# A decoder block: the rotation table's chain of the first half recorded twelve products sooner, and one convolved row's low part taken on VectorE

## The chip, the cores and the metric

The kernel runs on one core of a Trainium2 chip. The metric is the device time of one execution in microseconds (us), as the median of several runs. TensorE (PE in the profile, PEld for its weight loads) does the matrix products, VectorE (DVE), ScalarE (ACT) and GpSimd (POOL) do what is elementwise, and SyncE (SP) issues most transfers. ScalarE's queue issues some transfers too. Each engine carries out its instructions in the order in which they were recorded, and it waits where an operand or a buffer isn't ready yet.

## What is computed

The reference is one residual decoder block over a sequence of 2048 tokens of width 1024, in float32. What matters here, cut from it:

```python
h = rms_norm(x, g_norm[l]) * (1.0 + scale[:, None, :]) + shift[:, None, :]
proj = h @ w_in[l]
x_rnn, z_rnn, q, k, v, z_attn, g_r, g_a = jnp.split(proj, IN_SPLITS, axis=-1)
xc = causal_depthwise_conv(x_rnn, conv_w[l], conv_b[l])
hr = rg_lru(xc, w_a[l], b_a[l], w_x[l], b_x[l], lam[l], positions)
qh = apply_partial_rope(q.reshape(B, S, N_HEADS, HEAD_DIM), cos, sin)
kh = apply_partial_rope(k.reshape(B, S, N_HEADS, HEAD_DIM), cos, sin)
...
ang = positions.astype(jnp.float32)[..., None] * inv_freq
cos = jnp.cos(ang)[:, :, None, :]
sin = jnp.sin(ang)[:, :, None, :]
```

After the projection come a convolution of width 4 and a gated recurrence on one branch, attention with three dilations on the other, and a merge with two more projections.

## The kernel before, in words

**Products.** Every float32 matrix product is made of three products of two parts. An operand's high part is its value rounded to the matrix engine's format (`hi_act`, a copy on ScalarE, line 160), and the low part is the rest (`lo_pool`, a subtraction on GpSimd, line 166, or `lo_dve`, the same on VectorE, line 169). The three products are high by high, high by low and low by high (`mm3`).

**Halves and pairs.** The projection is made in two halves of 1024 tokens, `f` = 0 and 1. In each half the columns of `w_in` are worked through in pairs of 128-column blocks, and each pair takes seven products instead of eight, by a Strassen scheme (`strassen`). A product is twelve matmuls into one of the PSUM tiles X, Z, W, V or Y. Its order is X, then the last product of the pair before, into that pair's V, then Z, W, V, X again, and Y. The tiles come free by evictions: u1 is X's copy on ScalarE (line 391), and it has to be done before the second product into X starts. The sums with u2 and u3 leave by VectorE (`total`, line 461), and V has to be read before the next product into V.

**What sets the order.** Nothing is scheduled by a tool in this stage: the work of a pair is recorded in the order of the program, and after each product the program records what was set down for that product's number (`run_late`, with the tables `late` and `after_prod`, and `pump` for the weight operands). The weights of a product are loaded on SP's queue into five R tiles, summed on VectorE (lines 290, 291, 299, 304) and split into S tiles on ScalarE and GpSimd four products ahead; ScalarE's queue stores each S tile for the second half.

**The recurrence.** Eight of the pairs in a half are those of the recurrence (`recurrent`, m = 0 to 7). Their X parts go through the steps of `x_part`, at fixed lags in products: the convolution's first tap on ScalarE (line 974), three more on VectorE (980), the split of the convolved row xc into xh (160) and xl (166), the gates' six matmuls from it into the tiles pg, two sigmoids, decay, exponentials, a square root (1013), the scan on VectorE (1018) and the product with z (1023). The split is recorded two products after its start, and the gates' matmuls five after it. `j` is the column block of 512 tokens in the half. The pairs between those of the recurrence belong to the gates (`gate_pairs`, with a sigmoid in line 1235 or 1237 and, for z, a product in line 1242) or to the part of q and k that isn't rotated (`plain_pairs`).

**The rotation table.** `rotary_tables(rp, f)` sets down the chain that makes the cosines and sines of the half: a small load of the positions on SP (1047), a conversion (1054), the angles (1057), two reductions of the angle by multiples of two pi (1063 and 1070, on tiles kk and an of 128 by 128), a clamp, four sine activations on ScalarE with their own table (1084), a transposition on VectorE (1088), and eight stores to the scratch tabD on SP's queue (1092), in two groups of four. One step goes with each product, from product number `TABLES` of the half on. The two tiles of 128 by 512 that hold the result come from the ring `ev` in the first half, and so do the tiles in which the evicted gates wait for their stores. The table is read from tabD when the half's last pairs, the rotated ones, begin.

Of the kernel before, what the change touches and what calls it, by code (L numbers as in the profile page):

```python
# [11 lines left out]
F32R = mybir.dt.float32r  # L12
# [25 lines left out]
REBUILT = 20  # L38
NEG = 1e30

TABLES = 24

KV = (2, 3), (4, 3), (4, 3), (4, 3)

# [46 lines left out]
def decoder_block(ctx, tc, x, c, positions, g_norm, w_mod, b_mod, w_in, b_gate, conv_w, conv_b,  # L91
# [4 lines left out]
    def T(pool, shape, dt, tag, **kw):  # L96
        cnt[0] += 1
        return pool.tile(shape, dt, tag=tag, name=f"{tag}_{cnt[0]}", **kw)
# [60 lines left out]
    def hi_act(o, i):  # L159
        nc.scalar.activation(o, i, AF.Copy)  # L160
# [4 lines left out]
    def lo_pool(o, i, h):  # L165
        nc.gpsimd.tensor_tensor(o, i, h.bitcast(F32), ALU.subtract)  # L166
# [57 lines left out]
    n_prod, late, after_prod = [0], {}, {}  # L224
# [230 lines left out]
    def total(dst, ps, u, perm=lambda ap: ap):  # L455

        with tc.high_priority():
            if u is None:
                nc.scalar.activation(dst, perm(ps[:]), AF.Copy)
            else:  # L460
                nc.vector.tensor_tensor(dst, perm(ps[:]), perm(u[:]), ALU.add)  # L461
# [466 lines left out]
    def recurrent(rp, bigr, f, m):  # L928
# [33 lines left out]
        def x_part(j, ps, u):  # L962
            xr = T(rp, [P, 3 + CH], F32, "xr", bufs=2)
            total(xr[:, 3:].rearrange("p (j r) -> p j r", r=4), ps, u, nat)
            v = {}

            def new(tag, dt=F32, bufs=1):
                v[tag] = T(rp, [P, CH], dt, tag, bufs=bufs)
                return v[tag][:]

            def tap():
                nc.scalar.activation(xr[:, 0:3], xtail[:, m, :], AF.Copy)
                nc.scalar.activation(xtail[:, m, :], xr[:, CH : CH + 3], AF.Copy)
                nc.scalar.activation(new("xc", bufs=2), xr[:, 0:CH], AF.Identity, scale=cw(0),  # L974
                                     bias=par[:, C_CB + m : C_CB + m + 1])

            def taps():
                xc = v["xc"][:]
                for i in range(1, 4):
                    nc.vector.scalar_tensor_tensor(xc, xr[:, i : i + CH], cw(i), xc, ALU.mult, ALU.add)  # L980

            def split():
                hi_act(new("xh", F32R), v["xc"][:])
                lo_pool(new("xl", F32R), v["xc"][:], v["xh"][:])

            def gates():
                for gt in range(2):
                    v["p", gt] = T(pg, [P, CH], F32, "pg")
                    mm3(v["p", gt][:], w["h"][:, gt, :], w["l"][:, gt, :], v["xh"][:], v["xl"][:])

            def sigmoids():
                for gt, dst, cb in ((0, new("y", bufs=2), C_BA), (1, new("gi"), C_BX)):
                    nc.scalar.activation(dst, v["p", gt][:], AF.Sigmoid, bias=par[:, cb + m : cb + m + 1])

            def decay():
                gi, y = v["gi"][:], v["y"][:]
                nc.gpsimd.tensor_tensor(gi, gi, v["xc"][:], ALU.mult)
                nc.vector.scalar_tensor_tensor(y, y, sp8[:, m : m + 1], bigr[:, j * CH : (j + 1) * CH],
                                               ALU.mult, ALU.add)

            def exponentials():
                y, a, t = v["y"][:], new("a"), new("t")
                nc.scalar.activation(t, y, AF.Tanh)
                nc.scalar.activation(a, y, AF.Exp, scale=-1.0)
                nc.scalar.activation(y, a, AF.Square)

            def root():
                t = v["t"][:]
                nc.vector.scalar_tensor_tensor(t, v["y"][:], 1.0, t, ALU.add, ALU.mult)

            def square_root():
                t = v["t"][:]
                nc.scalar.activation(t, t, AF.Sqrt)

            def scan():
                y, t = v["y"][:], v["t"][:]
                nc.vector.tensor_tensor(t, t, v["gi"][:], ALU.mult)
                nc.vector.tensor_tensor_scan(y, v["a"][:], t, htail[:, m : m + 1], ALU.mult, ALU.add)

            def finish():  # L1020
                nc.scalar.activation(htail[:, m : m + 1], v["y"][:, CH - 1 : CH], AF.Copy)
                z4 = zs[j][:].rearrange("p (r j) -> p r j", r=4)
                nc.vector.tensor_tensor(z4, v["y"][:].rearrange("p (j r) -> p r j", r=4), z4, ALU.mult)

            def store():
                c0 = f * HALF + j * CH
                nc.sync.dma_start(yaT[m * P : (m + 1) * P, c0 : c0 + CH], zs[j][:])

            if j == 0:
                start[0] = n_prod[0]  # L1030
            steps_after(start[0] + 7 * j, (
                (0, tap), (1, taps), (2, split), (GATES, gates), (GATES + 1, sigmoids), (GATES + 2, decay),
                (GATES + 3, exponentials), (GATES + 4, root), (GATES + 5, square_root), (GATES + 6, scan),
                (GATES + 7, finish), (GATES + 7, store)))
# [6 lines left out]
    def rotary_tables(rp, f):  # L1041

        v = {}

        def angles():
            pi = T(rp, [P, 2, 4], I32, "pi")
            nc.sync.dma_start(pi[:], positions[0].rearrange("(n j r) -> j n r", n=NB, r=4)[:, 2 * f : 2 * f + 2, :])
            v["pi"] = pi
            for tag in ("an", "kk", "co"):
                v[tag] = T(rp, [P, 8, 16], F32, tag)  # L1050

        def convert():
            v["pf"] = T(rp, [P, 8], F32, "pf")
            nc.vector.tensor_copy(v["pf"][:], v["pi"][:].rearrange("p n r -> p (n r)"))

        def products():
            nc.vector.tensor_tensor(
                v["an"][:], v["pf"][:].unsqueeze(2).broadcast_to([P, 8, 16]),
                cs[:, K_IF : K_IF + 128].rearrange("p (b f) -> p b f", f=16), ALU.mult)

        flat = lambda tag: v[tag][:].rearrange("p b f -> p (b f)")
        magic = 1.5 * 2.0 ** 23
        tensor = lambda dst, src, s1, s2, *ops: lambda: nc.vector.tensor_scalar(flat(dst), flat(src), s1, s2, *ops)

        def reduce(per, bits, n):
            yield tensor("kk", "an", float(1 / per), None, ALU.mult)
            yield tensor("kk", "kk", magic, None, ALU.add)
            yield tensor("kk", "kk", -magic, None, ALU.add)
            for cc in split_const(per, bits, n):
                yield lambda cc=cc: nc.vector.scalar_tensor_tensor(flat("an"), flat("kk"), -cc, flat("an"), ALU.mult, ALU.add)  # L1070

        def shifted():
            nc.vector.scalar_tensor_tensor(flat("co"), flat("an"), math.pi / 2, flat("kk"), ALU.add, ALU.add)

        lim = 3.1415925
        quarter = (tensor("kk", "an", math.pi / 2, -float(TWO_PI), ALU.is_gt, ALU.mult), shifted,
                   *(tensor(tag, tag, lim, -lim, ALU.min, ALU.max) for tag in ("an", "co")))

        def sines():
            w = v["w"] = (raw_tile([P, KH, P]) if f else T(rp, [P, 4, P], F32, "ev", bufs=3))[:].rearrange("p k m -> p (k m)")  # L1080
            for i, (tag, first) in enumerate((("co", 1.0), ("an", -1.0))):
                rows = w[:, i * 2 * P : (i + 1) * 2 * P].rearrange("p (b h f) -> p b h f", b=8, h=2)
                for h, sign in ((0, first), (1, 1.0)):
                    nc.scalar.activation(rows[:, :, h, :], v[tag][:], AF.Sin, scale=sign)

        def turn():
            t = v["t"] = (raw_tile([P, KH, P]) if f else T(rp, [P, 4, P], F32, "ev", bufs=3))[:].rearrange("p k m -> p (k m)")
            nc.vector.transpose(t, v["w"])

        def store(i):  # L1090
            for q in range(4):
                nc.sync.dma_start(tabD[f, i].rearrange("d (b p j) -> p d b j", b=8, p=4)[q],
                                  v["t"][q * 32 : (q + 1) * 32, i * 2 * P : (i + 1) * 2 * P].rearrange("p (b j) -> p b j", b=8))

        at_, base = TABLES, n_prod[0]
        for fn in (angles, None, convert, products, *reduce(TWO_PI * 4096, 7, 8), *reduce(TWO_PI, 11, 5), *quarter, None, sines,
                   turn, lambda: store(0), lambda: store(1)):
            if fn:
                after_prod.setdefault(base + at_, []).append(fn)
            at_ += 1  # L1100
# [833 lines left out]
    v = {}  # L1934
# [297 lines left out]
```

## Time and profile before

| what | value |
|---|---|
| median of 3 runs | 2160.59 us (2159.23 to 2162.57) |
| the profiled execution | 2161.23 us, its span 2159.4 us |
| granted TensorE clock | 0.998 |
| VectorE, ScalarE, GpSimd busy | 68%, 60%, 52% of the span |
| the products of the first half's pairs | from about 124.7 us of the span on |
| VectorE busy, 206 to 226 us | 19.77 of 20 us |

In a list of instructions (the timeline) each row has the start in the span, the duration, the engine, the line, and the tile written and those read; "x12" merges twelve alike, and the bracket at the end gives the idle time of the engine before the instruction and what ended it. SPq and ACTq are transfers' issues. A row of the waits has the total, the number of times and the longest. A row of a line's or a tile's instructions has shortest, median and longest duration in ns.

### The profile page before, as it was taken

What the parts mean: (1) busy time and instruction counts of PE and PEld (TensorE: products, weight loads), DVE (VectorE), ACT (ScalarE), POOL (GpSimd) and SP (SyncE); (2) the same over time, 40 slices, a digit from 0 to 9 for tenths busy, and PEclk for the clock granted to TensorE, in tenths of its full rate; (3) what the DMA queues carried; (4) which work ended last, traced back from release to release, by engine and by line L of the source; (5) the groups of instructions that cost most, each with busy time, mean ns of one, the idle gap of its engine ahead of it and who ended that gap; (6) DMA issues with size and microseconds to landing.
All of it is one profiled execution on the core that took longest, in us unless ns stands there. A gap on an engine that the chain in (4) does not pass through costs nothing.

```text
span 2159.4 us, 32571 instructions
## 1 busy us (share of the span) xinstructions
PE 2136.6 (99%) x10539; PEld 1788.3 (83%) x10539; DVE 1463.3 (68%) x2582; ACT 1296.2 (60%) x2592; POOL 1120.6 (52%) x868
## 2 busy tenths in 40 slices
PE   9999999999999999999999999999999999999998
PEld 6888778888888888888888887889898988878887
DVE  6759878768656715544436684587777687788777
ACT  5748668668644527457457532677788888443333
POOL 1467667777666423223223675466666664432555
PEclk9999999999999999999999999999999999999999
DMA  8467887887655368899997676888887777899543
GB/s 301 142 211 256 280 290 264 288 294 244 174 115 166 108 229 291 301 305 311 323 318 240 152 173 171 300 269 263 273 275 218 256 236 239 300 316 300 181 170 114
DMA packets 416575, 521.39 MB, mean 241 GB/s; under 512 B 107574, under 2 KB 282898, under 8 KB 415380
## 3 DMA queue, kind: packets, MB, share of 16 engines
q1 hardware_dynamic: 376388, 401.65, 59.7%
q10 hardware_dynamic: 34384, 99.78, 12.2%
q0 software_dynamic: 5632, 17.88, 2.6%
q8 instruction: 83, 1.36, 0.3%
q14 instruction: 88, 0.72, 0.1%
HBM read 332.02 MB, written 187.17 MB: 240 GB/s over the span
## 4 chain that ended last, share of the span: by engine, by line
PE 71%; DVE 4%; DMA 3%; issue 1%; POOL 1%; ACT 1%; SPq 0%; ACTq 0%; POOLq 0%; DVEq 0%
PE X L152 14%; PE V L152 13%; PE pj L152 12%; PE Z L152 7%; PE W L152 7%; PE Y L152 6%; PE sc L152 4%; PE o L152 4%; PE pg L152 1%; PE pT L1568 1%; PE pT L1581 1%; DMA fg<-gaT 1%; DMA kraw<-kqT 1%; DVE ptl L169 1%; DVE yl L169 1%
## 5 line engine op out<-in xcount | busy, mean ns | idle before, releaser
L166 POOL TENSOR_TENSOR S<-R,S 128x512 fp32r<-128x512 f32 x192 | 295.3, 1546 | 169.3 <-ACT S L160 82.9
L152 PE MATMUL V<-T,S 128*128 128x512 f32 x1344 | 324.3, 390 | 1.9 <-DVE ev L461 1.9
L152 PE MATMUL X<-T,S 128*128 128x512 f32 x1344 | 323.8, 390 | 1.6 <-ACT u L391 1.3
L152 PE MATMUL pj<-yh,S 128*128 128x512 f32 x896 | 321.6, 402 | 1.3 <-DVE fg L1795 0.8
L152 PEld LDWEIGHTS X<-T,S 128*128 128x128 f32 x1344 | 251.8, 188 | 56.5 <-ACT u L391 2.9
L152 PEld LDWEIGHTS V<-T,S 128*128 128x128 f32 x1344 | 251.9, 188 | 55.9 <-issue 1.9
L166 POOL TENSOR_TENSOR S<-s,S 128x512 fp32r<-128x512 f32 x116 | 173.3, 1494 | 150.1 <-ACT S L160 114.3
L152 PEld LDWEIGHTS pj<-yh,S 128*128 128x128 f32 x896 | 168.3, 188 | 32.3 <-DVE S L169 1.3
L1481 ACT ACTIVATE pp<-pp,st 128x256 f32<-128x256 f32 (+3 forms) x256 | 133.8, 524 | 78.0 <-DVE st L1480 77.4
L152 PE MATMUL pj<-yl,S 128*128 128x512 f32 x448 | 175.5, 392 | 1.0 <-POOL yl L166 1.0
L160 ACT ACTIVATE S<-s 128x512 fp32r<-128x512 f32 x124 | 77.3, 624 | 145.1 <-DVE s L291 92.1
L152 PE MATMUL W<-T,S 128*128 128x512 f32 x672 | 161.6, 389 | 0.0
L152 PE MATMUL Y<-T,S 128*128 128x512 f32 x672 | 161.6, 389 | 0.0
L152 PE MATMUL Z<-T,S 128*128 128x512 f32 x672 | 161.4, 389 | 0.0
L160 ACT ACTIVATE S<-R 128x512 fp32r<-128x512 f32 x200 | 121.5, 622 | 59.0 <-DMA R<-in_w_in_dram 14.8
L169 DVE TENSOR_TENSOR ptl<-pT,pth 128x384 fp32r<-128x384 f32 (+1 forms) x160 | 97.8, 628 | 80.5 <-ACT pth L160 78.4
L152 PEld LDWEIGHTS W<-T,S 128*128 128x128 f32 x672 | 126.0, 188 | 26.9 <-issue 0.9
L152 PEld LDWEIGHTS Z<-T,S 128*128 128x128 f32 x672 | 126.2, 188 | 26.2
L152 PEld LDWEIGHTS Y<-T,S 128*128 128x128 f32 x672 | 126.1, 188 | 26.1
L166 POOL TENSOR_TENSOR s<-R,s 128x512 fp32r<-128x512 f32 x32 | 43.2, 1350 | 188.8 <-ACT s L160 164.6
L980 DVE SCALAR_TENSOR_TENSOR xc<-xr,par,xc 128x512 f32<-128x512 f32 x96 | 102.0, 1062 | 52.1 <-ACT xc L974 49.9
L1548 ACT ACTIVATE pp<-pp,M 128x256 f32<-128x256 f32 (+3 forms) x256 | 118.0, 523 | 12.8 <-DVE M L1680 12.8
(419 smaller groups left out, 4906.0 us busy)
## 6 DMA issues: line engine op xcount, KB each, us to landing
sD<-S ACTq DMA_DIRECT2D x140, 512.0 KB, 3.7
S<-sD SPq DMA_DIRECT2D x140, 512.0 KB, 5.0
S<-wD SPq DMA_DIRECT2D x82, 512.0 KB, 5.5
R<-in_w_in_dram SPq DMA_DIRECT2D x144, 256.0 KB, 3.3
wD<-s ACTq DMA_DIRECT2D x64, 256.0 KB, 5.1
kraw<-kqT SPq DMA_DIRECT2D x32, 384.0 KB, 5.1
T<-in_w_mod_dram SPq DMA_DIRECT2D x16, 512.0 KB, 9.1
vN<-ev SPq DMA_DIRECT2D x32, 256.0 KB, 2.7
```

Source lines behind the costliest of these rows:

```text
L152: nc.tensor.matmul(o, lhsT=l, rhs=r, start=st, stop=sp, **kw)
L160: nc.scalar.activation(o, i, AF.Copy)
L166: nc.gpsimd.tensor_tensor(o, i, h.bitcast(F32), ALU.subtract)
L169: return nc.vector.tensor_tensor(o, i, h.bitcast(F32), ALU.subtract).ins
L980: nc.vector.scalar_tensor_tensor(xc, xr[:, i : i + CH], cw(i), xc, ALU.mult, ALU.add)
L1481: nc.scalar.activation(pdst, pdst, AF.Exp, bias=m_, scale=-1.0, accum_out=l_)
L1548: nc.scalar.activation(pp, pp, AF.Copy, scale=w)
L1568: nc.tensor.transpose(pt[:, c0 + j * P : c0 + (j + 1) * P], pp[i][:, k * P : (k + 1) * P], ident)
L1581: nc.tensor.transpose(pt[:, c * P : (c + 1) * P], pp[:, half * P : (half + 1) * P], ident)
```

## The change

The rotation table's chain starts at product 12 of the first half instead of 24; in the second half it stays at 24. And the low part of one convolved row, that of m = 1, j = 0 in the first half, is subtracted on VectorE instead of on GpSimd. No other instruction changes.

```diff
-TABLES = 24
+TABLES = (12, 24)
...
-                lo_pool(new("xl", F32R), v["xc"][:], v["xh"][:])
+                (lo_dve if (f, m, j) == (0, 1, 0) else lo_pool)(new("xl", F32R), v["xc"][:], v["xh"][:])
...
-        at_, base = TABLES, n_prod[0]
+        at_, base = TABLES[f], n_prod[0]
```

What stands on the engines is shown here by rows of the recorded program, without times. First, VectorE from the gate rows of the first gate pair to the eviction of the second recurrent pair's z (zs from V). Before, in this stretch nothing of the table stands there:

```order
L1242 SCALAR_TENSOR_TENSOR ev_1565<-sg_1589,X_1412 128x512
L1242 SCALAR_TENSOR_TENSOR ev_1597<-sg_1619,ev_1597 128x512
L304 TENSOR_TENSOR s_274_1504<-R_267_1476,s_274_1504 128x512
L461 TENSOR_TENSOR ev_1645<-V_1513,u_269_1479 128x512
...
L397 TENSOR_TENSOR u_315_1711<-W_1674,u_307_1671 128x512
L299 TENSOR_TENSOR R_286_1563<-R_281_1535,R_286_1563 128x512
L461 TENSOR_TENSOR zs_1737<-V_1713,u_315_1711 128x512
```

Now, on the same engine and in the same stretch (pf, an and kk are the table's tiles):

```order
L1242 SCALAR_TENSOR_TENSOR ev_1570<-sg_1594,X_1412 128x512
L1054 CAST pf_1626<-pi_1559 128x8
L1242 SCALAR_TENSOR_TENSOR ev_1602<-sg_1624,ev_1602 128x512
L1057 TENSOR_TENSOR an_1561<-pf_1626,cs_60 128x128
L304 TENSOR_TENSOR s_274_1504<-R_267_1476,s_274_1504 128x512
...
L1063 TENSOR_SCALAR kk_1562<-kk_1562 128x128
L290 TENSOR_TENSOR s_317_1713<-R_290_1568,R_297_1600 128x512
...
L1063 TENSOR_SCALAR kk_1562<-kk_1562 128x128
L299 TENSOR_TENSOR R_290_1568<-R_281_1535,R_290_1568 128x512
L461 TENSOR_TENSOR zs_1748<-V_1723,u_320_1721 128x512
```

Five instructions of the table stand ahead of that eviction; the first step on kk, ahead of line 392, lies in the part left out.

Second, VectorE around the split of the convolved row of m = 1, j = 0, before:

```order
L980 SCALAR_TENSOR_TENSOR xc_1765<-xr_1761,par_61,xc_1765 128x512 x3
L461 TENSOR_TENSOR zs_1799<-Y_1767,u_315_1711 128x512
L1009 SCALAR_TENSOR_TENSOR t_1781<-y_1726,t_1781 128x512
L304 TENSOR_TENSOR s_313_1704<-R_305_1668,s_313_1704 128x512
L461 TENSOR_TENSOR xr_1844<-V_1713,u_307_1671 128x512
L1017 TENSOR_TENSOR t_1781<-t_1781,gi_1727 128x512
```

And now, with the low part xl and three steps on the angles among them (a fourth step stands ahead of line 980):

```order
L980 SCALAR_TENSOR_TENSOR xc_1777<-xr_1773,par_61,xc_1777 128x512 x3
L1070 SCALAR_TENSOR_TENSOR an_1561<-kk_1562,an_1561 128x128
L461 TENSOR_TENSOR zs_1812<-Y_1779,u_320_1721 128x512
L1009 SCALAR_TENSOR_TENSOR t_1793<-y_1736,t_1793 128x512
L169 TENSOR_TENSOR xl_1830<-xc_1777,xh_1828 128x512
L1070 SCALAR_TENSOR_TENSOR an_1561<-kk_1562,an_1561 128x128 x2
L304 TENSOR_TENSOR s_318_1714<-R_310_1677,s_318_1714 128x512
L461 TENSOR_TENSOR xr_1859<-V_1723,u_312_1680 128x512
L1017 TENSOR_TENSOR t_1793<-t_1793,gi_1737 128x512
```

The subtraction has left GpSimd's list and stands on VectorE right behind the root's step of line 1009. From the next scan to the eviction of the first part of the third gate pair (the gate that goes to gaT), VectorE's list holds ten steps of the table where it held seven.

Third, SP's queue where the stores of the table stand now, among the weight loads of the third recurrent pair; before, they stood thirteen rows further on, in two groups of four with a load and a store between them:

```order
L261 DMA R_425_2320<-in_w_in_dram 128x4x128
L261 DMA R_430_2347<-in_w_in_dram 128x4x128
L261 DMA R_438_2382<-in_w_in_dram 128x4x128
L1092 DMA tabD<-ev_2376 256x1x32 x8
L261 DMA R_449_2454<-in_w_in_dram 128x4x128
L261 DMA R_463_2513<-in_w_in_dram 128x4x128
```

All eight stores go together now, and a plain pair follows instead of a gate pair. On ScalarE, the sine activations with their table load stand ahead of the third recurrent pair's x (line 459), and the sigmoid behind them has to load its own table again: ScalarE's list is longer by that one load.

## Prediction

> **What bounds the kernel now.** I read the page's first part, then TensorE's waits in the stretch in which the first half's table is made, then the timeline there, engine by engine.
>
> ```profile
> span 2159.4 us, 32571 instructions
> PE 2136.6 (99%) x10539; PEld 1788.3 (83%) x10539; DVE 1463.3 (68%) x2582; ACT 1296.2 (60%) x2592; POOL 1120.6 (52%) x868
> ```
>
> TensorE is busy for 99% of the span and its matmuls stay the same, so the change can only open or close TensorE's gaps. All idle time together is 2159.4 - 2136.6 = 22.8 us. These are the two longest kinds of gap between 100 and 440 us:
>
> ```profile
> PE V L152 <- DVE ev L461: 1.9, 2, 1.5
> PE X L152 <- ACT u L391: 1.3, 2, 1.0
> ```
>
> Here the gaps are in TensorE's timeline, a third kind ahead of them, with the starts around each:
>
> ```profile
> 193.01 0.39 PE L152 MATMUL pg<-xh,gh 128*128 128x512 f32 x1
> 194.16 0.50 PE L152 MATMUL pg<-xl,gh 128*128 128x512 f32 x1 [0.76 <-POOL xl L166]
> 194.50 0.40 PE L152 MATMUL pg<-xh,gl 128*128 128x512 f32 x1
> 194.74 0.40 PE L152 MATMUL pg<-xh,gh 128*128 128x512 f32 x1
> ...
> 216.13 2.91 PE L152 MATMUL V<-T,S 128*128 128x512 f32 x12
> 219.35 3.02 PE L152 MATMUL X<-T,S 128*128 128x512 f32 x12 [0.31 <-ACT u L391]
> 222.21 2.88 PE L152 MATMUL Y<-T,S 128*128 128x512 f32 x12
> ...
> 235.81 2.88 PE L152 MATMUL V<-T,S 128*128 128x512 f32 x12
> 239.69 3.04 PE L152 MATMUL X<-T,S 128*128 128x512 f32 x12 [1.00 <-ACT u L391]
> 242.57 2.88 PE L152 MATMUL Y<-T,S 128*128 128x512 f32 x12
> ...
> 294.34 2.88 PE L152 MATMUL W<-T,S 128*128 128x512 f32 x12
> 298.69 3.00 PE L152 MATMUL V<-T,S 128*128 128x512 f32 x12 [1.46 <-DVE ev L461]
> ...
> 304.48 2.88 PE L152 MATMUL Y<-T,S 128*128 128x512 f32 x12
> 307.20 2.88 PE L152 MATMUL X<-T,S 128*128 128x512 f32 x12
> ```
>
> A product without a wait starts 2.72 us after the one before (304.48 to 307.20), and a gate matmul 0.24 us after its neighbour (194.50 to 194.74). What a gap really costs is the distance of the starts around it, less these steps:
>
> - B, the convolved row of m = 1: 193.01 to 194.50 is 1.49, less 2 x 0.24: **1.0 us**.
> - D, u1 late: 216.13 to 222.21 is 6.08, less 5.44: **0.6 us**.
> - E, u1 late again: 235.81 to 242.57 is 6.76, less 5.44: **1.3 us**.
> - F, V not evicted: 294.34 to 304.48 is 10.14, less 8.16: **2.0 us**.
>
> Together that is 4.9 us, or 0.23% of the time: no more than this can come back. A measurement of this kernel can tell about 0.2% (4.3 us) from no change.
>
> **The split on VectorE (B).**
>
> ```profile
> 189.03 0.61 ACT L160 ACTIVATE xh<-xc 128x512 fp32r<-128x512 f32 x1
> 192.83 1.28 POOL L166 TENSOR_TENSOR xl<-xc,xh 128x512 fp32r<-128x512 f32 x1
> ```
>
> xh is there at 189.64, yet GpSimd comes to xl only at 192.83, behind other work, and ends it at 194.11. TensorE wants it at 193.01 + 0.24 = 193.25. VectorE has xl right behind the root's step, so it starts at about 189.7 plus VectorE's delay, and it may take up to the 1.28 us of GpSimd's. B closes, -1.0 us, unless VectorE is more than 193.25 - 189.7 - 1.28 = 2.3 us behind by then. But these microseconds stay only if nothing later resynchronises TensorE, and E does: there TensorE waits for ScalarE, whose work hangs on VectorE.
>
> ```profile
> 182.51 0.63 ACT L956 ACTIVATE sg<-zs 128x512 f32<-128x512 f32 x1 [1.17 <-DVE zs L461]
> ...
> 193.43 0.63 ACT L1013 ACTIVATE t<-t 128x512 f32<-128x512 f32 x1
> ...
> 226.12 0.72 ACT L1237 ACTIVATE ev<-ev,par 128x512 f32<-128x512 f32 x1 [1.37 <-DVE ev L461]
> ...
> 239.07 0.58 ACT L391 ACTIVATE u<-X 128x512 f32<-128x512 f32 x1
> ```
>
> Read backwards from E: u1 ends at 239.65. ScalarE worked without a break since 226.12, when VectorE's eviction released it. VectorE worked without a break since 194.06, when the square root ended (193.43 + 0.63). ScalarE came to that without a break from 182.51, where VectorE's eviction of zs released it. So this chain, and not TensorE, sets when E ends. A TensorE that arrives 1.0 us sooner at D and E waits 1.0 us longer there. I count B's gain as nought up to E, and count what moves the chain instead.
>
> **The table's steps on VectorE (the unknown).** Ahead of 182.51 stand five steps more: the conversion, the angles, three on kk. Between the square root and 226.12 stand ten (seven on an, three on kk) where there were seven: the conversion, the angles, three on kk, two on an. The four steps and xl between 182.51 and the square root fall where VectorE waited for ScalarE anyway; I cost them at nothing, and if that cover is gone they join the chain. The durations:
>
> ```profile
> L1070 DVE SCALAR_TENSOR_TENSOR an<-kk,an x13: 259/294/1382, 222.4 to 263.6; 128x128 f32<-128x128 f32 x13
> L1063 DVE TENSOR_SCALAR kk<-kk x4: 712/1242/1315, 212.4 to 252.2; 128x128 f32<-128x128 f32 x4
> L1063 DVE TENSOR_SCALAR kk<-an x3: 217/218/1318, 212.2 to 266.1; 128x128 f32<-128x128 f32 x3
> L1054 DVE CAST pf<-pi x2: 171/714/1256, 206.2 to 856.6; 128x8 f32<-128x8 int32 x2
> ```
>
> A step takes 0.2 to 0.3 us at best and 1.3 at worst. The seven took about 1.26 + 0.22 + 2 x 1.24 + 3 x 0.29 = 4.8 us (the angles like a step on an).
>
> - Lowest: 0.17 + 0.26 + 3 x 0.22 = 1.1 ahead of zs, and 7 x 0.26 + 3 x 0.22 - 4.8 = -2.3 after it: -1.2 us.
> - By medians: 0.71 + 0.29 + 0.22 + 2 x 1.24 = 3.7 ahead, and 7 x 0.29 + 0.22 + 2 x 1.24 - 4.8 = -0.1 after: 3.6 us.
> - Highest: the conversion and every step on kk long ahead, 1.26 + 0.29 + 3 x 1.32 = 5.5 us; after it half of the ten long, 5 x 1.32 + 5 x 0.26 - 4.8 = 3.1: 8.6 us.
>
> The long ones are waits for GpSimd, as this shows:
>
> ```profile
> 169.44 1.75 POOL L166 TENSOR_TENSOR xl<-xc,xh 128x512 fp32r<-128x512 f32 x1
> ...
> 169.95 1.78 DVE L304 TENSOR_TENSOR s<-R,s 128x512 f32<-128x512 f32 x1
> ...
> 273.88 0.68 DVE L304 TENSOR_TENSOR s<-R,s 128x512 f32<-128x512 f32 x1
> ```
>
> The same sum takes 0.68 us when it begins before GpSimd's work and 1.78 when it begins within it, ending 0.54 us after GpSimd (171.19). A wait that a table step takes over is partly one that the next sum would have had, so I take a little over half of the medians, **+2.1 us**, for the delay at E. The Trainium skill ("SBUF — State Buffer", "SBUF: two separate sides") says that the shared port pair is an exclusive lock for the whole instruction, so that the later engine "fully blocks". The two rows agree. By that rule each inserted step would cost a GpSimd instruction wherever GpSimd is backlogged, which is the slower rival below.
>
> **The stores of the table (F).**
>
> ```profile
> 288.80 3.36 SPq L1092 DMA_DIRECT2D tabD<-ev x4
> ...
> 297.85 0.69 DVE L461 TENSOR_TENSOR ev<-V,u 128x512 f32<-128x512 f32 x1 [1.41 <-PE W L152]
> ```
> ```profile
> tabD<-ev SPq DMA_DIRECT2D x8, 32.0 KB, 3.7
> ```
>
> The profile names the product into W, which had nothing to do with this eviction. It needs an ev tile, and the tile that comes round is the one that tabD's stores read: the last issue ends at 292.16, the median landing takes 3.7 us and some take longer, and the gate pair evicts at once. Now the transposition stands behind the taps of the third recurrent pair (the row whose xl stands at 253.42 below), so it comes at about 253 to 255 us, and SP has its gap there:
>
> ```profile
> 245.44 3.53 SPq L261 DMA_DIRECT2D R<-in_w_in_dram  x2
> ```
> ```profile
> 259.58 1.08 SPq L261 DMA_DIRECT2D R<-in_w_in_dram  x2
> ```
>
> Eight issues at 3.36 / 4 = 0.84 us end by about 262 and land by 266 to 268. The plain pair takes that tile for its Y part, evicted shortly before the sum that stands at 273.88 above, at about 272. F closes: **-2.0 us**, at least the 1.46 that were idle. The weight loads queued behind the stores start 2 to 3 us later; their splits stand some five products of 2.72 off, so this costs nothing.
>
> **The sines on ScalarE.**
>
> ```profile
> 278.99 1.28 ACT L1084 ACT_TABLE_LOAD   x1
> ...
> 280.70 0.50 ACT L1084 ACTIVATE ev<-an 128x128 f32<-128x128 f32 x2
> ```
> ```profile
> 253.42 1.29 POOL L166 TENSOR_TENSOR xl<-xc,xh 128x512 fp32r<-128x512 f32 x1
> ...
> 256.40 0.39 PE L152 MATMUL pg<-xl,gh 128*128 128x512 f32 x1
> ```
>
> They take 281.20 - 278.99 = 2.2 us and now stand ahead of the third recurrent pair's x. Its xl ended at 254.71 and was wanted at 256.40, a slack of 1.7, so TensorE waits about **+0.5 us** more there (0 to 2.2). The further table load (1.28) stands behind xh, where ScalarE has idle time. The Trainium skill ("ScalarE: Activation LUTs", "What ACT_TABLE_LOAD costs") has about 1380 ns of drain behind the 1283 ns of a load. By it the wait would be 1.9 us and the sum 1.4 us higher. The rows show 1.28 us and an end 2.2 us after the start, four activations included; the measurement decides.
>
> **The sum.** +2.1 (chain at E) + 0.5 (sines) - 2.0 (F) = +0.6 us. The profiled execution took 2161.23 us, so it would be 2161.8. The median of the runs shown, 2160.59, gives **2161.2 us**, within 0.2%.
>
> **The rivals.**
>
> - *The chain keeps its pace.* The steps hide, VectorE and ScalarE come to E 1.0 us sooner with TensorE, and B and F come back: -3.0, 2157.6 us. For it: VectorE idle before the square root, and 1.28 us less on GpSimd. Against it: VectorE is busy 19.77 of 20 us after 206. Within 0.2% as well.
> - *All four gaps close*, since the chain of steps ends sooner: -4.9, 2155.7 us, faster. It needs D and E closed too; but ten steps now stand where seven stood.
> - *Slower: each inserted step waits for a whole GpSimd instruction.* Then E is delayed by 8.6 us: +8.6 + 0.5 - 2.0 = +7.1, 2167.7 us. It decides from a delay of 4.3 + 2.0 - 0.5 = 5.8 us on. TensorE would show it earlier too, with u1 late in the second recurrent pair or V late at 185. For it: the two rows of line 304. Against it: most of the 13 steps on an took 0.29.
> - *The split does not do what it says:* VectorE comes to xl over 2.3 us late and B stays. That alone changes nothing at E and lies within the forecast.
>
> **How the numbers follow.** The even trade (a delay at E up to 5.8 us): 0.58, with the fourth rival in it. The chain keeps its pace: 0.22. All closed: 0.08. Each step waits: 0.12. So faster by over 0.2%: 0.08, within: 0.80, slower: 0.12. The range goes from 2157.0, a little below the second case, to 2165.5, which takes in delays up to 6.4; it leaves out the third case and most of the slower one, 0.08 + 0.10.
>
> **What would show it.** B gone, with xl on VectorE ended before the gate's second matmul is due; F gone, with tabD's issues near 255 to 262. Right for the chain: X still waits for u1 at D and E, for longer than 0.3 and 1.0. Wrong: no wait for u1 there and a time under 2157, or waits for u1 or V already before 190 us and a time over 2165.5. The sines' step is right if the gates' matmuls of m = 2 wait for xl by a few tenths.

## The result and the profile after

| what | before | after |
|---|---|---|
| median, 16 runs each | 2160.48 us (2158.81 to 2164.77) | 2164.09 us (2161.74 to 2166.77) |
| the profiled execution, its span | 2161.23 us, 2159.4 us | 2163.14 us, 2161.3 us |

The ratio is 1.0016, with a 95% interval from 1.0009 to 1.0023. The changed kernel is slower by 3.6 us between the medians (1.9 to 5.0 by the interval), which is within the 0.2% of the forecast (4.3 us); only the upper end of the interval lies beyond it. The time lies in the predicted range, and 2.9 us above the predicted 2161.2.

These are TensorE's longest waits between 100 and 440 us in the changed kernel (total, times, longest):

```profile
PE V L152 <- DVE xr L461: 3.3, 1, 3.3
PE X L152 <- ACT u L391: 1.4, 1, 1.4
PE pg L152 <- POOL xl L166: 0.7, 1, 0.7
PE V L152 <- DVE ev L461: 0.5, 1, 0.5
```

The first kind is new: V waits for xr, the eviction of the second recurrent pair's V. The wait for xl is another row's than before (m = 2), and the 0.5, at 402.93 us, was there before too, at 400.54. TensorE's timeline of the changed kernel, with the starts around the four gaps that the prediction named:

```profile
193.49 0.39 PE L152 MATMUL pg<-xh,gh 128*128 128x512 f32 x1
...
193.94 0.40 PE L152 MATMUL pg<-xh,gl 128*128 128x512 f32 x1
...
198.32 3.02 PE L152 MATMUL V<-T,S 128*128 128x512 f32 x12 [3.29 <-DVE xr L461]
...
218.88 2.91 PE L152 MATMUL V<-T,S 128*128 128x512 f32 x12
...
224.61 2.88 PE L152 MATMUL Y<-T,S 128*128 128x512 f32 x12
...
238.21 2.88 PE L152 MATMUL V<-T,S 128*128 128x512 f32 x12
242.51 3.04 PE L152 MATMUL X<-T,S 128*128 128x512 f32 x12 [1.42 <-ACT u L391]
245.39 2.88 PE L152 MATMUL Y<-T,S 128*128 128x512 f32 x12
...
258.99 0.39 PE L152 MATMUL pg<-xh,gh 128*128 128x512 f32 x1
260.11 0.50 PE L152 MATMUL pg<-xl,gh 128*128 128x512 f32 x1 [0.73 <-POOL xl L166]
260.45 0.39 PE L152 MATMUL pg<-xh,gl 128*128 128x512 f32 x1
...
298.26 2.88 PE L152 MATMUL W<-T,S 128*128 128x512 f32 x12
301.09 3.00 PE L152 MATMUL V<-T,S 128*128 128x512 f32 x12
...
306.87 2.88 PE L152 MATMUL Y<-T,S 128*128 128x512 f32 x12
```

Read by distances of starts, as in the prediction:

- B is closed: 193.49 to 193.94 is 0.45 where it was 1.49, so 1.0 us came back. It is lost again right behind these matmuls, in the gap of 3.29 ahead of V.
- D, 218.88 to 224.61, is 5.73, less 5.44: 0.3 us instead of 0.6. TensorE comes there 2.75 us later than before (216.13), so u1 hardly holds it up.
- At E, the product into Y starts at 245.39 where it started at 242.57: the delay there is **2.8 us**. TensorE had 2.4 of them already when it came to E (238.21 instead of 235.81), out of the wait ahead of V; the wait for u1 adds 0.4.
- The third recurrent pair's gates, 258.99 to 260.45, take 1.46 for 0.48: **1.0 us** that wasn't there.
- F, 298.26 to 306.87, is 8.61, less 8.16: 0.45 instead of 2.0, so **1.5 us** came back.

2.8 + 1.0 - 1.5 = 2.3, and the product at 306.87 does stand 2.4 us later than before (304.48). Little changes after that in this pair of profiles: the spans differ by 1.9 us. So the 3.6 us of the medians are 2.4 that the rows show and 1.2 that no row shows, and 2.4 lies inside the interval. The two profiled executions lie 0.75 us above and 0.95 us below their medians, so the pair can't show the whole.

Where the 3.3 us come from stands in VectorE's timeline, here of the changed kernel:

```profile
189.63 0.69 DVE L461 TENSOR_TENSOR zs<-Y,u 128x512 f32<-128x512 f32 x1
190.23 1.10 DVE L1009 SCALAR_TENSOR_TENSOR t<-y,t 128x512 f32<-128x512 f32 x1
191.25 1.78 DVE L169 TENSOR_TENSOR xl<-xc,xh 128x512 fp32r<-128x512 f32 x1
192.95 2.68 DVE L1070 SCALAR_TENSOR_TENSOR an<-kk,an 128x128 f32<-128x128 f32 x2
195.56 1.75 DVE L304 TENSOR_TENSOR s<-R,s 128x512 f32<-128x512 f32 x1
197.23 1.04 DVE L461 TENSOR_TENSOR xr<-V,u 128x512 f32<-128x512 f32 x1
198.19 0.80 DVE L1017 TENSOR_TENSOR t<-t,gi 128x512 f32<-128x512 f32 x1
```

And the same stretch of the kernel before:

```profile
188.02 0.69 DVE L461 TENSOR_TENSOR zs<-Y,u 128x512 f32<-128x512 f32 x1
188.62 0.68 DVE L1009 SCALAR_TENSOR_TENSOR t<-y,t 128x512 f32<-128x512 f32 x1
189.22 1.23 DVE L304 TENSOR_TENSOR s<-R,s 128x512 f32<-128x512 f32 x1
190.38 1.09 DVE L461 TENSOR_TENSOR xr<-V,u 128x512 f32<-128x512 f32 x1
194.16 1.75 DVE L1017 TENSOR_TENSOR t<-t,gi 128x512 f32<-128x512 f32 x1 [2.69 <-POOL xl L166]
```

Before, VectorE stood idle for 2.69 us behind xr; that was the cover on which the prediction counted. (The bracket names xl on GpSimd, which L1017 doesn't read; of what it reads, the root's t came last, at 194.06.) Now xr ends at 198.27 instead of 191.47, 6.8 us later: 1.6 because zs is that much later already (1.4 of it come from the five steps ahead of 182.51), 0.4 for the root's longer step, 1.7 for xl, 2.6 for the two steps on the angles, 0.5 for the longer sum of line 304. The 2.69 are used up, and L1017 follows without a gap, 4.0 us later. It doesn't wait for the square root, which ended 2.8 us before:

```profile
194.78 0.63 ACT L1013 ACTIVATE t<-t 128x512 f32<-128x512 f32 x1
```

### The profile page after: what moved, and what is told of

Its sections match the earlier page's. It is cut to its first block, busy times and chain, and to the rows that moved or that the text cites. A ratio compares the mean times of both kernels' runs of the same rounds, so it can differ in the third digit from the quotient of the medians.

```text
span 2161.3 us, 32575 instructions
## 1 busy us (share of the span) xinstructions
PE 2136.2 (99%) x10539; PEld 1787.7 (83%) x10539; DVE 1464.6 (68%) x2583; ACT 1297.6 (60%) x2593; POOL 1119.2 (52%) x867
## 4 chain that ended last, share of the span: by engine, by line
PE 70%; DVE 4%; DMA 3%; issue 2%; POOL 1%; ACT 1%; SPq 0%; ACTq 0%; POOLq 0%; DVEq 0%
PE X L152 14%; PE V L152 14%; PE pj L152 11%; PE Z L152 7%; PE W L152 7%; PE Y L152 6%; PE sc L152 4%; PE o L152 3%; PE pg L152 1%; PE pT L1568 1%; PE pT L1581 1%; DVE ptl L169 1%; DMA kraw<-kqT 1%; DVE yl L169 1%; DMA fg<-gaT 1%
```

## The experiments

Theory, after this reading: VectorE's steps between zs and xr (xl and two on the angles) are long because each waits for an instruction of GpSimd, which is backlogged there; they hold up xr, and with it TensorE. Rivals: the two parts of the change are independent and the loss is the row's or the table's alone; or the five steps ahead of the eviction of zs set the delay, and those behind it don't; or the steps' number doesn't matter, since they only take over a wait that the next sum would have had.

**One part alone: the table.** The chain starts at 12, the row's low part is on GpSimd as before.

```diff
-                (lo_dve if (f, m, j) == (0, 1, 0) else lo_pool)(new("xl", F32R), v["xc"][:], v["xh"][:])
+                lo_pool(new("xl", F32R), v["xc"][:], v["xh"][:])
```

> The chain starts at product 12 as in the changed kernel, but the low part of the convolved row of m = 1 stays on GpSimd. Theory (what stands on VectorE between the root's step and the eviction xr makes TensorE's V wait, and each of these instructions waits for a whole GpSimd instruction): the two steps on an still stand there, xl doesn't, so xr comes about 1.8 us sooner and the 3.3 us wait of V goes; the gate's second matmul waits for xl on GpSimd again, by 1 to 2 us; the wait for u1 at E (X near 242.5 us) comes 1 to 2 us sooner than in the changed kernel, and the time is 1 to 2 us below the changed kernel's 2164.1, near 2162.6. Rival (the five steps ahead of zs set the delay): E and the time stay within 0.5 us of the changed kernel.

Measured: 2163.96 us (11 runs), 1.0010 [1.0001, 1.0018] of before. The gates wait for xl again, and E is as in TensorE's timeline:

```profile
195.24 0.50 PE L152 MATMUL pg<-xl,gh 128*128 128x512 f32 x1 [1.26 <-POOL xl L166]
...
242.06 3.01 PE L152 MATMUL X<-T,S 128*128 128x512 f32 x12 [1.03 <-ACT u L391]
```

The wait of V for xr is gone. The time is that of the changed kernel within what can be told, and E is only 0.45 us sooner than in it (242.06 against 242.51): the 1 to 2 us expected there didn't come, and E and the time are as the rival with the five steps had them. VectorE's rows show where the lead went. Its scan (line 1018) starts at 197.47 us, 1.6 sooner than in the changed kernel. But GpSimd is at work beside the next instructions, so the step on the angles behind the scan takes 1.32 us, not 0.26, and line 1023 takes 1.49, not 1.05. The next eviction of V, at 206.86, is 0.08 sooner. The table's move alone makes a loss of this order, even without the wait of V for xr.

**The other part alone: the row.** The chain starts at 24, the row's low part is on VectorE.

```diff
-TABLES = (12, 24)
+TABLES = (24, 24)
```

> Only the low part on VectorE; the chain at product 24 as before. Theory: xl ends by about 191.5 us, xr by 193.5, no wait of the gates and none of V there; but TensorE waits at D and E until ScalarE's u1, at the same times as before, so B's 1.0 us is given back at E; F (1.5 us idle near 298.7) stays. Time within 0.5 us of the 2160.5 before. Rival (the subtraction on VectorE is itself what delays xr): V waits for xr by 1 us or more and the time is 1 us or more above before. Second rival (TensorE's gain stays): X after E starts 1.0 us sooner than 242.57 and the time is 2159.5.

Measured: 2159.71 us (12 runs), 0.9994 [0.9986, 1.0003]. VectorE's timeline and then TensorE's:

```profile
189.50 0.78 DVE L169 TENSOR_TENSOR xl<-xc,xh 128x512 fp32r<-128x512 f32 x1 [0.37 <-ACT xh L160]
190.20 1.78 DVE L304 TENSOR_TENSOR s<-R,s 128x512 f32<-128x512 f32 x1
...
193.97 0.96 DVE L1017 TENSOR_TENSOR t<-t,gi 128x512 f32<-128x512 f32 x1 [0.98 <-ACT t L1013]
```
```profile
238.74 3.04 PE L152 MATMUL X<-T,S 128*128 128x512 f32 x12 [0.97 <-ACT u L391]
...
297.98 2.97 PE L152 MATMUL V<-T,S 128*128 128x512 f32 x12 [1.71 <-DVE ev L461]
```

Here xl takes 0.78 us, not 1.78, and VectorE still has 0.98 us of idle time behind xr: the cover holds. B is closed, and its 1.0 us survives E, as this run's second rival had it: X starts there at 238.74 instead of 239.69, with the same wait. The prediction had said that a TensorE that comes sooner only waits longer at E. X does still wait for u1 there, but the chain that sets u1 has itself become shorter: L1017 takes 0.96 instead of 1.75 (the row of before above). In both kernels it ends 0.55 us after the instruction that GpSimd has beside it, a split of S, which ends at 194.39 here and at 195.35 before, since xl no longer stands ahead of it.

**The two steps out of the way.** As the changed kernel, but the chain pauses for two products, so that no step on the angles stands between xl and xr (`steps` is the list of the chain's steps).

```diff
...
+        if f == 0:
+            steps[9:9] = [None, None]
...
```

> The changed kernel with a pause of two products in the chain, so that the two steps on an no longer stand between xl and xr; everything behind comes two products later. Theory: xr comes 2.7 us sooner, V's wait falls from 3.3 to about 0.6 us; E's X starts 1 to 2.5 us sooner than 242.5; F stays closed; time 1 to 2.5 us below the changed kernel, near 2162.3. Rival (the five steps ahead of zs): V's wait becomes smaller but E's X stays within 0.5 us of 242.5, since the chain there is as late as before, and the time stays near 2164.

Measured: 2162.62 us (11 runs), 1.0004 [0.9996, 1.0013]. TensorE's timeline:

```profile
195.65 3.02 PE L152 MATMUL V<-T,S 128*128 128x512 f32 x12 [0.76 <-DVE xr L461]
...
240.93 3.02 PE L152 MATMUL X<-T,S 128*128 128x512 f32 x12 [1.01 <-ACT u L391]
```

V's wait falls from 3.29 to 0.76 us, by 2.5 us for two steps that took 2.6; E is 1.6 us sooner than in the changed kernel (242.51). The steps had not merely taken over another's wait, and steps behind zs do count, against the rival with the five steps. In the time the gain is not shown, since the two intervals overlap (1.0004 here, 1.0016 for the changed kernel).

**The two steps twice.** As the changed kernel, with one more step of the same form behind each of the two, on a tile that is written anew before it is read (added work).

```diff
...
+            for i in (9, 10):
+                def twice(fn=steps[i]):
+                    fn()
+                    nc.vector.scalar_tensor_tensor(flat("co"), flat("kk"), -1.0, flat("an"), ALU.mult, ALU.add)
+                steps[i] = twice
...
```

> The changed kernel with each of the two steps on an between xl and xr followed by one more of the same size (128 by 128, two operands in SBUF) whose result is overwritten later. Theory (each waits for a whole GpSimd instruction): V's wait goes from 3.3 to about 5.9 us and the time up by about 2.6, near 2166.7. Rival (a step costs its own 0.3 us and the long ones are something else): V's wait 3.9 us and the time 2164.7.

Measured: 2165.79 us (11 runs), 1.0019 [1.0010, 1.0027]; V waits 4.75 us. VectorE's timeline, and GpSimd's beside it:

```profile
192.96 1.38 DVE L1070 SCALAR_TENSOR_TENSOR an<-kk,an 128x128 f32<-128x128 f32 x1
194.38 1.26 DVE L1102 SCALAR_TENSOR_TENSOR co<-kk,an 128x128 f32<-128x128 f32 x1
195.67 1.24 DVE L1070 SCALAR_TENSOR_TENSOR an<-kk,an 128x128 f32<-128x128 f32 x1
196.94 1.24 DVE L1102 SCALAR_TENSOR_TENSOR co<-kk,an 128x128 f32<-128x128 f32 x1
198.10 0.68 DVE L304 TENSOR_TENSOR s<-R,s 128x512 f32<-128x512 f32 x1
```
```profile
192.45 1.74 POOL L166 TENSOR_TENSOR S<-s,S 128x512 fp32r<-128x512 f32 x1
194.16 1.32 POOL L166 TENSOR_TENSOR S<-R,S 128x512 fp32r<-128x512 f32 x1
195.45 1.31 POOL L960 TENSOR_TENSOR zs<-zs,sg 128x512 f32<-128x512 f32 x1
196.72 1.31 POOL L166 TENSOR_TENSOR S<-R,S 128x512 fp32r<-128x512 f32 x1
199.57 1.28 POOL L166 TENSOR_TENSOR S<-s,S 128x512 fp32r<-128x512 f32 x1 [1.54 <-ACT S L160]
```

Every step ends about 0.15 us after an instruction of GpSimd's (194.34 after 194.19, 195.64 after 195.48, 196.91 after 196.76, 198.18 after 198.03). The two engines take turns, one instruction each, as long as GpSimd has work. When it runs out at 198.03, the sum of line 304 takes 0.68 us where it took 1.75. So V's wait grew by 1.5 us, between the 2.6 of the theory and the 0.6 of the rival: each step costs a whole turn, and a wait that the next sum would have had goes away once GpSimd has run out of work. GpSimd goes on at 199.57, though, and L1017 then takes 1.75 us instead of 0.80; the scan starts at 201.43, 2.4 us later than in the changed kernel. The times don't tell the two kernels apart (1.0019 and 1.0016).

**The tail later (F).** In the first half the sines, the transposition and the stores come four products later, once with the row as before (start 24) and once with the row on VectorE.

```diff
...
-*quarter, None, sines,
+*quarter, None, *([] if f else 4 * [None]), sines,
...
```

> The kernel before (chain at product 24, low part on GpSimd), with a pause of four products ahead of the sines in the first half, so that the table's stores come behind the last eviction of the gate pair. Theory (at F, V waits because the eviction needs the ev tile that the table's stores still read): the wait of V near 298.7 us closes, 1.5 to 2.0 us, all other waits stay; time near 2158.8. Rival (the eviction waits for something else, as the profile names the product into W): the wait stays and so does the time, 2160.5.

> The chain at product 24, its tail four products later as in the run beside it, and the low part of the one row on VectorE. Theory: the row's part is worth what it was alone (0.5 to 1.0 us) and F's 1.5 to 2.0 come on top: time near 2158.0, 2 to 3 us below before. Rival (both gains meet the same later wait, so that only one counts): no more than the run beside it.

Measured: 2161.54 us, 0.9998 [0.9989, 1.0007], and 2160.53 us, 0.9996 [0.9987, 1.0005] (11 runs each). Of the idle 1.46 us at F, 0.84 and 0.83 stay, although the table's stores are issued only from 295.38 and 294.26 us on. This doesn't speak against the tile that the prediction named, for the pause also changes which of the three ev tiles comes round. By the recorded programs, the eviction at F needs, in the kernel before, the tile that the second four stores of the table read. The last of these is issued at 291.0 us and takes 6.7 to land: 297.7, and the eviction starts at 297.85. With the tail later it needs the tile of the gate pair's Y part, whose store to zaT is issued at 293.9 and takes 3.4: 297.3, and the eviction starts at 297.36 (292.7, 3.4 and 296.22 with the row on VectorE). So the two runs only put one store in the place of another. In the changed kernel the tile's last store, also to zaT, is issued at 292.70, and the eviction comes at 300.27. In the profile the tail alone ends 2.0 us sooner than before, but only 0.5 of it is there at 304 us; the rest, and the medians, are within the spread of the runs.

**The chain elsewhere.** Row on VectorE, the chain much later in the half: the table is read only at 575 us.

```diff
-TABLES = (12, 24)
+TABLES = (75, 24)
```

The other kernels of this kind have 66, 100, 110 and 118 there.

> The changed kernel with the chain at product 75 of the first half instead of 12 (so about 335 to 425 us, where TensorE has one gap of 0.5 us before), the low part on VectorE. Theory (the waits for u1 at D and E come from the chain's steps on VectorE there): D and E close with B and F, 4 to 5 us together; the chain opens some new waits at its new place, 0 to 2 us; time 2156 to 2158. Rival (ScalarE's own work makes u1 late at E): E keeps about 1 us and the time is 2157.5 or more; second rival (the chain costs the same wherever it lies): new waits of 3 us or more, time 2159 or more.

> As the run with the start at product 75, with the start at 66, so that the stores fall elsewhere among the gate pairs. Theory: D, E, B and F close as there; the stores may hold an ev tile that a gate's eviction needs, 0 to 2 us; time 2156 to 2159.

> The chain begins at the hundredth product instead of the twelfth (row's low part stays on VectorE), so its steps should stand from about 435 us on and its sines near 495; the table is first read at 575 us. In the kernel before TensorE has no idle time from 460 to 580 us. Theory 1 (a step costs TensorE time only where GpSimd is behind and VectorE decides; there is slack here): the waits at 193, 216, 236 and 295 us are gone or under 0.3 us, no new one over 0.5 us, 3 to 5 us sooner than before at 480 us, time 2156.0 to 2158.0. Theory 2 (a TensorE that is sooner meets evictions that are no sooner, wherever the chain stands): half comes back as new waits for V between 395 and 570 us, time 2158.5 to 2160.5.

> As with the start at the hundredth product, some 28 us later: steps from about 462 us on, sines near 524, stores near 540. Theory 1: the four old waits gone or under 0.3 us, no new one over 0.5 us, time 2156.0 to 2158.0. Theory 2: new waits for V between 395 and 570 us, time 2158.5 to 2160.5. Where both starts behave alike, the place within the stretch does not matter.

> The latest start of the three: steps from about 485 us on, sines near 547, stores near 563, just ahead of the table's first read at 575 us. Theory 1: as with the other two up to 560 us, time 2156.0 to 2158.0. Against it: the stores may hold up the reads of the table, which then begin later than 575 us and make the first rotated pair wait by 1 to 3 us, time 2158 to 2161.

| start | median | ratio to before, interval | waits of TensorE in the profile |
|---|---|---|---|
| 66 | 2160.96 us | 0.9998 [0.9989, 1.0006] | E 0.2; 1.62 and 1.05 for V at 398 and 411 us |
| 75 | 2162.39 us | 1.0003 [0.9994, 1.0012] | E 0.2; 0.96 for V at 397 and 0.97 at 460 us |
| 100 | 2160.25 us | 0.9996 [0.9987, 1.0006] | E 0.2; 1.34 for u1 at 562 us |
| 110 | 2161.30 us | 0.9999 [0.9990, 1.0008] | E 0.2; 1.13 for xl at 539 us, 1.34 for u1 at 563 us |
| 118 | 2165.24 us | 1.0023 [1.0014, 1.0032] | E 0.2; 2.11 and 1.99 for V at 541 and 562, 0.89 for u1 at 568 us |

All five close the gaps B and F and nearly close E, D keeps its wait of 0.3, and none is measurably faster; start 118 is slower. Start 100 shows best where the gain goes. TensorE's timeline there, and in the kernel before at the same instructions:

```profile
536.71 0.39 PE L152 MATMUL pg<-xh,gh 128*128 128x512 f32 x1
...
558.09 2.88 PE L152 MATMUL V<-T,S 128*128 128x512 f32 x12
562.32 1.89 PE L152 MATMUL X<-T,S 128*128 128x512 f32 x7 [1.34 <-ACT u L391]
```
```profile
541.17 0.39 PE L152 MATMUL pg<-xh,gh 128*128 128x512 f32 x1
...
561.62 2.66 PE L152 MATMUL V<-T,S 128*128 128x512 f32 x11
```

At 537 us TensorE is 4.5 us ahead of the kernel before. At 558 it is 3.5 ahead, and X, which started at about 564.34 before (561.62 and a product of 2.72), is 2.0 ahead, although no step of the table is left there (its stores' last issue begins at 508.0). ScalarE comes to that u1 only 1.3 us sooner than before:

```profile
561.69 0.57 ACT L391 ACTIVATE u<-X 128x512 f32<-128x512 f32 x1
```
```profile
563.01 0.58 ACT L391 ACTIVATE u<-X 128x512 f32<-128x512 f32 x1
```

Ten microseconds on, the product into Z starts at 573.87 for 575.29: 1.4 us are left of the 4.5. With start 110 it starts at 574.94, 0.35 ahead, where 4.2 us were gained up to the gates' first matmul (537.02 for 541.17). So theory 2 of these runs holds in its mechanism, though the waits there are mostly for u1 and not for V: between 537 and 575 us VectorE and ScalarE have little lead over TensorE, and when it comes sooner it meets them. (The profiled execution of start 100 is the quickest of its runs, 3.3 us shorter in its span than before; what it gains beyond the 1.4 lies behind this half, where nothing was changed.) With start 118 the expected reason, reads of the table held up by its stores, isn't what the trace shows; the transposition waits for a tile of the ring ev until a gate's store (grT) has landed, and the engines behind it wait along:

```profile
559.55 0.71 DVE L1088 STREAM_TRANSPOSE ev<-ev 128x512 f32<-128x512 f32 x1 [3.96 <-DMA grT<-ev]
```

## Why the prediction was right in the end, and where it wasn't

The forecast, no change within 0.2%, was right, and the measured time lies in the range. The mechanism named, a delay of the chain at E against what F gives back, was right too. It was not an even trade: +0.6 us lies below the interval (1.9 to 5.0), and all three terms came out 0.5 to 0.7 us worse than forecast. That the delay at E came so near its forecast is luck, as errors in it cancelled. One step failed.

- *"The four steps and xl between 182.51 and the square root fall where VectorE waited for ScalarE anyway; I cost them at nothing, and if that cover is gone they join the chain."* This step failed. The cover behind xr was 2.69 us; xr came 6.8 us later, so L1017 came 4.0 us later. The 6.8 are the 1.4 of the five steps ahead and 5.4 of what stands between, so what was costed at nothing cost 2.7. The trace had shown the cover's length, and I had not set it against the price of the steps. It also made a wait in a place that I had not named: V for xr at 195 us. Taking two of these steps away took 2.5 us of that wait away, and doubling them added 1.5. At E, though, 0.45 us and 1.6 were gained where xl or the two steps were away, since GpSimd takes part of the lead back behind the scan.
- *The delay at E, +2.1 us.* Measured 2.8, for partly wrong reasons. The eviction of zs of the second recurrent pair in the changed kernel, and before:

```profile
183.15 0.68 DVE L461 TENSOR_TENSOR zs<-V,u 128x512 f32<-128x512 f32 x1
```
```profile
181.79 0.69 DVE L461 TENSOR_TENSOR zs<-V,u 128x512 f32<-128x512 f32 x1
```

  Ahead of it the five steps cost 1.4 us where my medians gave 3.7 (the three on kk took 0.20 to 0.21 each, with GpSimd idle), and the covered steps cost 2.7 instead of nothing. L1017 itself was 0.95 shorter (0.80 instead of 1.75), which I had not foreseen, and from the scan to E the ten steps cost 0.3 less than the seven had, close to the 0.1 less of my medians. 1.4 + 2.7 - 0.95 - 0.3 = 2.8.
- *"X still waits for u1 at D and E, for longer than 0.3 and 1.0."* True at E (1.42), not at D, where the wait shrank, because TensorE had been held up by V before.
- *B.* It closed, as said, since VectorE was in time: xl ended at 193.03, due at 193.73. It took 1.78 us, though, and not the 1.28 that I gave as its most. "I count B's gain as nought up to E" came true in the changed kernel. Its reason, that TensorE only waits longer at E, left out that the row's move shortens the chain to E as well: with the row alone the 1.0 us stayed.
- *F, -2.0 us.* 1.5 came back, and no wait is left there. The tile was read rightly. The stores were issued from 257.77 us on, close to the 255 expected, and took longer, 8.11 us for the eight.
- *The sines, +0.5 us.* The gates of m = 2 lost 1.0, within 0 to 2.2. The profile doesn't separate the sines from the lateness that VectorE had by then.
- *The rival "each inserted step waits for a whole GpSimd instruction".* It is what happened in the stretch where GpSimd had work without a break. The Trainium skill ("SBUF — State Buffer", "SBUF: two separate sides") has the shared port pair as an exclusive lock held for the whole instruction; the turns in the kernel with the doubled steps agree, 1.24 to 1.38 us for a step. Where GpSimd is idle, the same step takes 0.26 to 0.29. A delay of 8.6 us at E didn't come because most of the steps stand in such places: nine of the fifteen that I priced took under 0.3 us.
- *The sum.* +2.1 + 0.5 - 2.0 = +0.6 was forecast, 2.8 + 1.0 - 1.5 = +2.3 is what the rows give. The even trade, as the prediction named it (a delay at E up to 5.8 us), takes this in.

What stays open: 1.2 us of the medians' difference, which no stage of the profiled pair shows, and how much of the 1.0 us at the gates of m = 2 is the sines'.

## What to carry to other kernels

Before inserted work is costed at nothing, the idle time that is to hide it is to be measured, and all that is put in front of it added up, at the long durations where GpSimd is backlogged. Gaps of the bounding engine are not a sum to be collected: of the 4.5 and 4.2 us closed with starts 100 and 110, 1.4 and 0.35 were left at 575 us, because TensorE had moved up to a place where its helpers had little lead. So count the lead of the helpers over the rest of the stage first. And a step's price is that of its place; beside a backlogged GpSimd the same step took over four times as long.

## What the runs showed of the hardware

- In the stretch where GpSimd had work without a break, VectorE and GpSimd alternated, one instruction each: a step of 128 by 128 elements took 1.24 to 1.38 us instead of 0.26 to 0.29, and the sum of line 304 took 1.75 to 1.78 instead of 0.68.
- With GpSimd out of work after four steps, the next sum took its short 0.68 us; when GpSimd had work again, L1017 took the long 1.75.
- Taking one instruction of 1.28 us from GpSimd made VectorE's L1017 0.8 us shorter (1.75 to 0.96) without any change to it.
